# A diagonal mask moved from a matmul to VectorE, and one more job ahead of the emptying of a queue

## The chip, the cores and the metric

The kernel runs on one core of a Trainium2 chip. The metric is the time of one execution in device microseconds (us). Engines are named PE (TensorE's matmuls; PEld its weight loads), DVE (VectorE), ACT (ScalarE), POOL (GpSimd) and SP (SyncE, which issues the DMAs).

## The reference

One decoder layer for 2048 tokens of width 1024, behind 16 learned meta tokens. One input projection gives q, k, v, forget logits and a gate for 16 attention heads of width 64, and the input and gate of a pooling branch. The attention's logits are causal and carry a decay:

```
h = layer_norm(concat([meta, x]))
q, k, v, f_logit, g_att, u, g_pool = split(h @ w_in)
c = cumsum(log_sigmoid(f_logit + b_forget))
s = q_t . k_s / 8 + c_t - c_s            # where key s <= query t, else -inf
a = (softmax(s) @ v) * silu(g_att)
p = multiscale_pool(u) * silu(g_pool)
out = layer_norm(2 ** 0.25 * h + concat([a, p]) @ w_out)[16:]
```

Everything is float32. The kernel keeps that precision with three matmuls of split operands (high x high, high x low, low x high) where one would do.

## The kernel before, in words

Only SP's queue is ordered by the framework's scheduler. On PE, DVE, ACT and POOL the instructions run in the order in which the code issues them (`Ordered`, lines 78 to 95). All helpers issue through line 86, so the profile shows L86 for every engine, and instructions are told apart by the names of their tiles.

The first stage normalises the tokens, turns them, and projects v. The second stage (about 333 to 1358 us) is a list of 40 jobs: two of the pooling branch, then the 16 `qk_job`s (one per head) with gate and pooling jobs between them, and three gate jobs (`ga_job`) behind the last head. Each job runs chunks through `proj` (line 490): 8 steps of three matmuls into a tile named `d`, which has two buffers. A `qk_job` has five chunks of 416 or 412 columns, a `ga_job` four of 512. ACT and DVE empty `d`; a `ga_job`'s result goes through one tile `gst` to DRAM (`gd`).

While the jobs run, a second kind of work is strewn between the steps. For every head and every block of 128 queries the kernel needs the row maximum of q.k, which the attention later subtracts. `max_piece` (line 502) makes it: one or two matmuls (`mx<-ka,qa`) put up to 1024 columns of logits into an accumulator tile `mx`, of which there are two buffers; on the block's diagonal, 128 columns, a mask must be added; then DVE reduces the columns to one maximum (`mxs<-mx`). A head has 26 such pieces, 16 of them with a diagonal, and `max_end` (line 525) adds five entries: two maxima on DVE, a transposition on PE (`tr`), the split of the result (`mh`, `ml`) and its store. The entries wait in a queue `pend`. After every step `tick` (line 478) adds to a credit and issues an entry for each whole credit: at least 0.3 a step, and, while `sched["tail"]` is set, the entries left divided by the steps left, so that the queue is empty by then.

`run_jobs` (line 682) runs jobs from n0 to n1. It is called up to the first job behind the last head; then the rest of `later` (products of the pooling branch, put off by one chunk) and of `pend` is issued at once, the pools of the second stage are closed, and the attention's first tiles are set up: memsets of `ka`, `vt`, `vc`, `zo`, `qa`, and loads of keys, values and queries (`load_kv`, `load_q`). Then `run_jobs` runs the other two gate jobs, and the third stage, the attention with the output projection strewn in, begins with `emit_s` (`s<-qa,ka`). The fourth stage is the rest of the output projection and the last normalisation.

In the job list `last_qk` is 36 of 0 to 39, so three gate jobs, 37 to 39, follow the last head.

Of the kernel before, what the change touches and what calls it, by code (L numbers as in the profile page):

```python
# [9 lines left out]
F32 = mybir.dt.float32  # L10
F32R = mybir.dt.float32r
BF16 = mybir.dt.bfloat16
AF = mybir.ActivationFunctionType
ALU = mybir.AluOpType
AX = mybir.AxisListType

P = 128
# [4 lines left out]
KT = D // P  # L22
# [18 lines left out]
def kernel(  # L41
# [20 lines left out]
    nc = tc.nc  # L62
# [35 lines left out]
    nc = NC()  # L98
    mm = nc.tensor.matmul
# [33 lines left out]
    def pool(stack, name, **k):  # L133
        if k.get("space") is not DRAM:
            k["reuse_waits"] = "tile"
        return stack.enter_context(tc.tile_pool(name=name, bufs=1, **k))

    cpool = pool(ctx, "cpool", side="right")
    ident = cpool.tile([P, P], F32, tag="ident", name="ident")
    make_identity(mk_ident, ident)  # L140
    identb = cpool.tile([P, P], BF16, tag="identb", name="identb")
    nc.vector.tensor_copy(identb, ident)
    mask_q = cpool.tile([P, P], BF16, tag="mask_q", name="mask_q")
    nc.gpsimd.memset(mask_q, 0.0)
    nc.gpsimd.affine_select(
        out=mask_q, in_=mask_q, compare_op=ALU.is_ge, fill=NEG, base=0,
# [5 lines left out]
        out=mask_k, in_=mask_k, compare_op=ALU.is_ge, fill=NEG, base=0,  # L152
# [16 lines left out]
    def dense():  # L169
        return psd.tile([P, 512], F32, tag="d", name="d", bufs=2)  # L170
# [13 lines left out]
    def w_split(st):  # L184
        wh, wl = w_slots()
        split(wh, wl, st, nc.gpsimd)
        return wh, wl

    with ExitStack() as vscope:
# [219 lines left out]
        out=tri, in_=tri, compare_op=ALU.is_ge, fill=0.0, base=-1,  # L409
# [3 lines left out]
        out=tri, in_=tri, compare_op=ALU.is_ge, fill=0.0, base=0,  # L413
# [4 lines left out]
    for c0, c1 in CHUNKS:  # L418
        n = c1 - c0
        ps = dense()  # L420
        for k in range(KT):
# [4 lines left out]
            out=zc[:, :n], in_=ps[32 : 32 + H, :n], func=AF.Identity, bias=bf_t  # L426
# [45 lines left out]
    ka = qp.tile([66, L], F32R, tag="ka", name="ka")  # L472
# [3 lines left out]
    sched = {"credit": 0.0, "steps": 0, "hook": None}  # L476
# [25 lines left out]
    def max_piece(mx, i, p):  # L502
        lo, hi = max(112, 1024 * p), min(1024 * (p + 1), P * i + 256)
        base = 1024 * p

        def go():
            ps = psm.tile([P, 1024], F32, tag="mx", name="mx", bufs=2)
            v = lo
            while v < hi:
                e = min(hi, 512 * (v // 512 + 1))  # L510
                diag = e == P * i + 256
                mm(
                    ps[:, v - base : e - base], qa[:, NM + P * i : NM + P * (i + 1)],
                    ka[:, v - 112 : e - 112], start=True, stop=not diag,
                )
                if diag:
                    mm(ps[:, e - P - base : e - base], identb, mask_q, start=False, stop=True)
                v = e
            nc.vector.tensor_reduce(
                out=mx[:, p, i : i + 1], in_=ps[:, lo - base : hi - base], axis=AX.X, op=ALU.max  # L520
            )

        return go
# [138 lines left out]
    jobs = [others.pop(0), others.pop(0)]  # L662
# [5 lines left out]
    last_qk = max(n for n, j in enumerate(jobs) if j[0] is qk_job)  # L668
    sched["tail"] = False

    def fetch(n):
        return w_load(jobs[n][2]) if n < len(jobs) else None
# [9 lines left out]
    def run_jobs(n0, n1):  # L682
        for n in range(n0, n1):
            fn, a, _ = jobs[n]

            def mid():
                if n + 1 < len(jobs):
                    state["w"] = w_split(state["st"])
                    state["st"] = fetch(n + 2)

            w = state.get("w") or cur
            if fn is not qk_job:
                m = n
                steps = 0
                while m < len(jobs) and jobs[m][0] is not qk_job:
                    steps += 40 if jobs[m][0] is u_job else 32
                    m += 1
                sched["steps"] = steps + KT
                sched["tail"] = True
            fn(a, w, mid)  # L700

    run_jobs(0, last_qk + 2)
    while later:
        later.popleft()()
    while pend:
# [85 lines left out]
    load_q(0)  # L791
    fetched[0] = 1
    kvq.popleft()
    run_jobs(last_qk + 2, len(jobs))
    phase_a.close()

    phase_w = ExitStack()
# [345 lines left out]
    for i, tt in enumerate(order):  # L1143
# [12 lines left out]
        for q in range(parts):  # L1156
            qs = slice(D // parts * q, D // parts * (q + 1))
            nc.vector.scalar_tensor_tensor(
                out=yt[:, qs], in0=yt[:, qs], scalar=mv[:, 0:1], in1=g_bc[:, qs],
# [3 lines left out]
                out=yt[:, qs], in0=yt[:, qs], scalar=rs, in1=b_bc[:, qs], op0=ALU.mult, op1=ALU.add  # L1163
# [63 lines left out]
```

## Time and profile before

| | |
|---|---|
| median of 3 runs | 2393.3 us (2392.06 to 2394.99) |
| the profiled execution | 2390.21 us, its span 2388.5 us |
| granted TensorE clock, mean | 0.993 |
| instructions | 32719 |
| PE busy | 2321.6 us, 97% |
| DVE busy | 1431.6 us, 60% |
| ACT, POOL busy | 959.7 us, 718.1 us |

How to read the rows. A timeline row gives start and duration in us, the engine, the operation, `out<-in` by the tiles' names, and the shape; in brackets the idle time of the engine before it and what ended it. `x2` merges two equal neighbours. A matmul's end is modelled and lies past the next one's start, so costs on PE are read from start to start. A tile's row gives the number of instructions and their shortest, middle and longest duration in ns, and the first and last start.

### The profile page before, as it was taken

What the parts mean: (1) busy time and instruction counts of PE and PEld (TensorE: products, weight loads), DVE (VectorE), ACT (ScalarE), POOL (GpSimd) and SP (SyncE); (2) the same over time, 40 slices, a digit from 0 to 9 for tenths busy, and PEclk for the clock granted to TensorE, in tenths of its full rate; (3) what the DMA queues carried; (4) which work ended last, traced back from release to release, by engine and by line L of the source; (5) the groups of instructions that cost most, each with busy time, mean ns of one, the idle gap of its engine ahead of it and who ended that gap; (6) DMA issues with size and microseconds to landing.
All of it is one profiled execution on the core that took longest, in us unless ns stands there. A gap on an engine that the chain in (4) does not pass through costs nothing. (4 is left out here: it accounts for less than half of the span.)

```text
span 2388.5 us, 32719 instructions
## 1 busy us (share of the span) xinstructions
PE 2321.6 (97%) x11706; PEld 1922.0 (80%) x11706; DVE 1431.6 (60%) x2116; ACT 959.7 (40%) x1813; POOL 718.1 (30%) x528
## 2 busy tenths in 40 slices
PE   6999999999999999999999999999999999999998
PEld 5778798898988989888887767777777777776787
DVE  6641145644655456545535188787888878778357
ACT  4431221222212212121111387777778777776000
POOL 4730021212313404050001135353453535444000
PEclk8999999999999999999999999999999999999999
DMA  7853231222222222222212576575666657555955
GB/s 255 263 164 97 59 96 61 89 63 82 90 61 90 77 66 85 68 75 86 77 67 79 159 205 190 159 222 164 195 187 198 199 164 227 175 176 152 310 185 167
DMA packets 317506, 333.59 MB, mean 140 GB/s; under 512 B 27744, under 2 KB 241072, under 8 KB 317312
## 3 DMA queue, kind: packets, MB, share of 16 engines
q1 hardware_dynamic: 317344, 331.51, 45.5%
q8 instruction: 92, 1.51, 0.3%
q14 instruction: 70, 0.57, 0.1%
HBM read 207.43 MB, written 124.00 MB: 139 GB/s over the span
## 5 line engine op out<-in xcount | busy, mean ns | idle before, releaser
L86 PE MATMUL d<-hh,wh 128*128 128x412 f32 (+2 forms) x1472 | 561.2, 381 | 0.0
L86 PE MATMUL d<-hl,wh 128*128 128x412 f32 (+2 forms) x1472 | 538.6, 366 | 0.0
L86 PE MATMUL d<-hh,wl 128*128 128x412 f32 (+2 forms) x1472 | 538.6, 366 | 0.0
L86 DVE TENSOR_REDUCE mxs<-mx 128x1 f32<-128x912 f32 (+14 forms) x416 | 358.1, 864 | 279.7 <-PE mx L86 275.2
L86 DVE TENSOR_TENSOR pl<-s,ph 128x512 fp32r<-128x512 f32 (+2 forms) x576 | 374.6, 663 | 166.6 <-ACT s L86 153.5
L86 ACT ACTIVATE ph<-s 128x512 fp32r<-128x512 f32 (+2 forms) x576 | 334.6, 581 | 170.1 <-PE s L86 159.2
L86 PE MATMUL d<-wh,xm 128*128 128x512 f32 x1024 | 352.3, 400 | 5.1 <-DMA xm<-xa 5.1
L86 ACT ACTIVATE s<-s 128x512 f32<-128x512 f32 (+2 forms) x576 | 332.7, 578 | 0.0
L86 PEld LDWEIGHTS d<-hl,wh 128*128 128x128 f32 x1472 | 278.4, 189 | 23.1
L86 PEld LDWEIGHTS d<-hh,wl 128*128 128x128 f32 x1472 | 276.9, 188 | 23.5
L86 PEld LDWEIGHTS d<-hh,wh 128*128 128x128 f32 x1472 | 280.6, 191 | 18.2
L86 PE MATMUL s<-qa,ka 68*128 68x512 f32 (+4 forms) x704 | 258.1, 367 | 18.4 <-DVE pl L86 18.3
L86 POOL TENSOR_TENSOR wl<-wst,wh 128x1024 fp32r<-128x1024 f32 x40 | 96.2, 2405 | 576.0 <-ACT wh L86 575.9
L86 PE MATMUL s<-qb,kb 128*128 128x512 f32 (+4 forms) x704 | 244.8, 351 | 0.0
L86 PE MATMUL xo<-ph,vt 128*128 128x512 f32 (+3 forms) x640 | 232.9, 368 | 0.0
L86 POOL TENSOR_TENSOR tu<-ph 128x512 f32<-128x512 f32 x144 | 191.3, 1330 | 134.6 <-ACT ph L86 116.1
L86 PEld LDWEIGHTS d<-wh,xm 128*128 128x128 f32 x1024 | 192.3, 189 | 42.8 <-issue 4.9
L86 PE MATMUL yo<-pl,vt 128*66 128x512 f32 (+3 forms) x640 | 223.0, 365 | 0.5 <-ACT c L86 0.5
L86 PE MATMUL mx<-ka,qa 66*128 66x512 f32 (+5 forms) x704 | 200.2, 351 | 6.5 <-ACT qa L86 3.9
L86 PE MATMUL d<-wl,xm 128*128 128x512 f32 x512 | 204.3, 399 | 0.0
L86 PEld LDWEIGHTS s<-qa,ka 68*128 68x128 f32 (+1 forms) x704 | 127.7, 181 | 73.3 <-DVE pl L86 31.3
L86 PEld LDWEIGHTS mx<-ka,qa 66*128 66x128 f32 x704 | 133.0, 190 | 23.5 <-ACT qa L86 5.2
(140 smaller groups left out, 3049.2 us busy)
## 6 DMA issues: line engine op xcount, KB each, us to landing
xm<-xp SPq DMA_DIRECT2D x32, 1024.0 KB
xm<-xa SPq DMA_DIRECT2D x20, 1024.0 KB
vd<-vs SPq DMA_DIRECT2D x32, 512.0 KB
vt<-vd SPq DMA_DIRECT2D x64, 256.0 KB
qb<-kqd SPq DMA_DIRECT2D x64, 256.0 KB
xa<-am SPq DMA_DIRECT2D x32, 512.0 KB
xp<-pm SPq DMA_DIRECT2D x32, 412.0 KB
kqd<-lo SPq DMA_DIRECT2D x64, 206.0 KB
```

Of the source, the lines that this page charges most:

```text
L86: return in_order(f(*a, **k))
```

## The change

The mask that is added to the diagonal's 128 columns was a bfloat16 tile, added by a matmul with the identity matrix (`identb`) into the accumulator. It becomes a float32 tile that DVE adds to the accumulator in place, between the block's last matmul and its reduction. And the first call of `run_jobs` goes on to the second job behind the last head, `drain` being `last_qk + 3`; the steps over which `tick` spreads the entries are counted up to `drain` where that comes before the next head. One job is left for the second call.

```diff
-    mask_q = cpool.tile([P, P], BF16, tag="mask_q", name="mask_q")
+    mask_q = cpool.tile([P, P], F32, tag="mask_q", name="mask_q")
...
-                    ka[:, v - 112 : e - 112], start=True, stop=not diag,
+                    ka[:, v - 112 : e - 112], start=True, stop=True,
                 )
                 if diag:
-                    mm(ps[:, e - P - base : e - base], identb, mask_q, start=False, stop=True)
+                    d = ps[:, e - P - base : e - base]
+                    nc.vector.tensor_tensor(out=d, in0=d, in1=mask_q, op=ALU.add)
...
-                while m < len(jobs) and jobs[m][0] is not qk_job:
+                while m < len(jobs) and jobs[m][0] is not qk_job and m != drain:
                     steps += 40 if jobs[m][0] is u_job else 32
                     m += 1
-                sched["steps"] = steps + KT
+                sched["steps"] = steps if m == drain else steps + KT
                 sched["tail"] = True
             fn(a, w, mid)
 
-    run_jobs(0, last_qk + 2)
+    drain = last_qk + 3
+    run_jobs(0, drain)
     while later:
         later.popleft()()
     while pend:
         pend.popleft()()
...
-    run_jobs(last_qk + 2, len(jobs))
+    run_jobs(drain, len(jobs))
```

## The prediction, made before any run of the change

> **What bounds the kernel now.** I read the busy shares of the page first, then the windows around the change, then the timeline of single matmuls.
>
> ```profile
> PE 2321.6 (97%) x11706; PEld 1922.0 (80%) x11706; DVE 1431.6 (60%) x2116; ACT 959.7 (40%) x1813; POOL 718.1 (30%) x528
> 333.00:1275.50 942.50, 938.64 (x4814) 838.89 (x4813) 491.99 (x671) 180.60 (x352) 210.51 (x165) 1.00 0.24 77
> 1275.50:1301.30 25.80, 25.80 (x117) 20.66 (x116) 9.20 (x11) 3.73 (x6) 2.40 (x1) 1.00 0.20 67
> 1301.30:1311.80 10.50, 6.52 (x20) 3.20 (x18) 9.09 (x12) 1.13 (x2) 2.51 (x2) 0.70 0.18 66
> 1311.80:1358.20 46.40, 46.39 (x194) 37.56 (x195) 1.82 (x6) 5.38 (x9) 5.13 (x6) 0.96 0.41 124
> ```
>
> The window lines give length, then busy PE, PEld, DVE, ACT, POOL, the granted clock, the DMA share, GB/s. From 333 to 1301 (projections, with the row maximum's pieces strewn between) PE has work all the time and DVE half of it: 491.99 of 942.50. So an instruction taken from PE there is worth its slot, and one given to DVE is free as long as DVE keeps up. The exception is 1301.30 to 1311.80: the pieces left over when the queue is emptied behind the first job after the last head. There DVE is full (9.09 of 10.50), PE waits, and its granted clock falls to 0.70.
>
> **The mask's matmul, removed.** There is one per head and block of 128 queries, 256 in all.
>
> ```profile
> L86 PE MATMUL mx<-mask_q,identb x256: 230/231/330, 333.1 to 1310.1; 128*128 128x128 bf16 x128
> 601.93 0.34 PE L86 MATMUL mx<-ka,qa 66*128 66x384 f32 x1
> 602.12 0.23 PE L86 MATMUL mx<-mask_q,identb 128*128 128x128 bf16 x1
> 602.16 0.43 PE L86 MATMUL d<-hh,wh 128*128 128x412 f32 x1
> 602.43 0.35 PE L86 MATMUL d<-hl,wh 128*128 128x412 f32 x1
> 602.62 0.35 PE L86 MATMUL d<-hh,wl 128*128 128x412 f32 x1
> ...
> 1272.08 0.58 PE L86 MATMUL mx<-ka,qa 66*128 66x400 f32 x2
> 1272.50 0.35 PE L86 MATMUL d<-hh,wh 128*128 128x412 f32 x1
> ...
> 1274.77 0.22 PE L86 MATMUL mx<-ka,qa 66*128 66x128 f32 x1
> 1274.83 0.23 PE L86 MATMUL mx<-mask_q,identb 128*128 128x128 bf16 x1
> 1274.87 0.43 PE L86 MATMUL d<-hh,wh 128*128 128x412 f32 x1
> 1275.14 0.35 PE L86 MATMUL d<-hl,wh 128*128 128x412 f32 x1
> ```
>
> A matmul's listed duration overlaps the next, so I go by starts. An undisturbed projection matmul of 412 columns takes 0.187 us (602.43 to 602.62; longer runs give the third digit), 0.454 ns a column. From 601.93 to 602.43 are 0.50 us; 384 columns are 0.174 and 412 are 0.187, so 0.139 is the mask's. Of this 0.04 is its own slot (602.12 to 602.16); the rest makes the next projection matmul late (0.27 instead of 0.187). At the narrowest piece, 1274.77 to 1275.14, 0.37 - 0.058 - 0.187 = 0.125. Done for the pieces whose rows stand alone, the same subtraction gives 0.131 as the middle value, whatever the width. A piece without a mask has no such loss: 1272.08 to 1272.50 is 0.42 for 912 columns, which at 0.454 ns are 0.414. So I take the whole 0.131: the 248 masks that start before 1275.5 give 248 x 0.131 = **32.5 us**. Ends: 248 x 0.04 = 9.9, if only the slot goes, and 248 x 0.14 = 34.7. I take the upper part because the piece without a mask is the case after the change.
>
> The Trainium skill ("TensorE: Matmul & The Clock Gate", the section "Wait — 56ns, not 53.3ns?") has a 128-column matmul cost 55.6 ns, start to start, on a warm array. By that alone the masks would give 248 x 0.056 = 13.9 us and the total below would shrink by 18.6; the rows show more than twice the page's price, so I go by the rows.
>
> **The add on VectorE, new.** 256 adds of 128 columns, in and out of the accumulator, with the mask from SBUF. No such row exists; the nearest are these:
>
> ```profile
> 1312.52 0.28 DVE L86 SCALAR_TENSOR_TENSOR ml<-tr,mh 16x128 fp32r<-16x128 f32 x1 [0.77 <-ACT mh L86]
> L86 DVE TENSOR_REDUCE mxs<-mx x416: 280/1028/1226, 333.3 to 1311.2; 128x1 f32<-128x912 f32 x54, 128x1 f32<-128x1024 f32 x11, 128x1 f32<-128x128 f32 x10, 128x1 f32<-128x144 f32 x6
> 1361.45 0.69 DVE L86 TENSOR_TENSOR pl<-s,ph 128x512 fp32r<-128x512 f32 x1 [46.94 <-ACT s L86]
> 1362.74 0.57 DVE L86 TENSOR_TENSOR pl<-s,ph 128x400 fp32r<-128x400 f32 x1 [0.60 <-ACT s L86]
> ```
>
> Two inputs, one from the accumulator, 128 columns: 0.28. The same kind at 512 and 400 columns extrapolates to 0.69 - 384 x 0.00107 = 0.28. I take 0.29: 248 x 0.29 = 71.9 us, DVE goes from 52% to 60% of 942.5. Behind the add on DVE stand the piece's reduction and whatever comes next (the low halves of k and q, the pool branch's two products); who waits for them is PE, at the matmul that reuses the buffer, two pieces on. The tightest place of the undisturbed part:
>
> ```profile
> 409.67 1.44 DVE L86 TENSOR_REDUCE mxs<-mx 128x1 f32<-128x912 f32 x2
> 411.22 0.58 PE L86 MATMUL mx<-ka,qa 66*128 66x400 f32 x2
> ```
>
> The first of the two reductions ends 1.11 after 409.67, at 410.78; PE reuses its buffer at 411.22: 0.44 to spare. Of the other distances before the tail, worked out for all 416 reductions, eleven lie under 0.8 us. In a replay of all rows, pushed back by 0.29 an add, and with each masked piece 0.131 sooner, no PE start is reached; with 0.8 an add it costs 1.9 us. So the adds cost **0**; if the cover were gone, the excess over about 0.6 an add would go to PE. The float32 mask is built once, by two instructions of GpSimd at the very start, ahead of the first projection; I count 0.
>
> **Two jobs ahead of the emptying, pieces spread over both.**
>
> ```profile
> 1275.52 0.40 PE L86 MATMUL d<-hh,wh 128*128 128x512 f32 x1
> ...
> 1303.97 3.18 DVE L86 TENSOR_REDUCE mxs<-mx 128x1 f32<-128x912 f32 x3
> 1305.13 2.22 PE L86 MATMUL mx<-ka,qa 66*128 66x400 f32 x4 [1.45 <-DVE mxs L86]
> 1311.81 0.38 PE L86 MATMUL tr<-ident,mxs 128*16 128x128 f32 x1 [1.39 <-DVE mxs L86]
> 1312.84 0.63 PE L86 MATMUL d<-hh,wl 128*128 128x512 f32 x1
> 1313.27 0.63 PE L86 MATMUL d<-hh,wh 128*128 128x512 f32 x1
> ...
> 1336.18 0.60 ACT L86 ACTIVATE gst<-d 128x512 f32<-128x512 f32 x1 [4.96 <-PE d L86]
> 1341.74 0.60 ACT L86 ACTIVATE gst<-d 128x512 f32<-128x512 f32 x1 [4.96 <-PE d L86]
> 1358.18 0.39 PE L86 MATMUL s<-qa,ka 68*128 68x512 f32 x1
> ```
>
> After the last head 22 entries are queued: 17 pieces and five of the end. The old rule shares them over 104 steps but runs only 32 of them, at the floor of 0.3 a step, so 10 pieces go out and 7, with the end, are left for the burst. The new rule shares them over 64 steps, all of which run: 22/64 = 0.34 a step, nothing is left. A pair of pieces then comes every six steps, 4.2 us, for at most 1.11 + 1.22 + 0.29 = 2.6 us of DVE.
>
> From the first job's start at 1275.52 to the attention's first matmul at 1358.18 are 82.66 us. Needed at full rate: 3 jobs x 4 chunks x 5.56 (1336.18 to 1341.74) = 66.7; the 17 pieces, 12928 columns by the code (912 for each of blocks 8 to 14, their second parts 4480, block 15's 2064), x 0.454 ns = 5.9; the transpose 0.2. That leaves **9.9 us** of waiting, slow clock (0.43 between 1312.84 and 1313.27 instead of 0.23) and the last 8 masks. Ends: 0, if the burst only moves, and 9.9.
>
> What moves behind it: the memsets of the attention's tiles (1.81 us the longest, on GpSimd), the loads of its first keys, values and queries on SP's queue, and the pool branch's last product on DVE.
>
> ```profile
> 1310.35 1.81 POOL L86 MEMSET ka<- 2x2064 f32 x1 [4.59 <-PE mx L86]
> 1314.41 0.32 SPq L86 DMA_DIRECT2D ka<-kqd  x1
> 1317.13 0.59 SPq L86 DMA_DIRECT2D qb<-kqd  x1
> 1337.66 0.56 SPq L86 DMA_DIRECT2D vc<-vd  x1
> ```
>
> The first set is issued 2.6 to 5.9 us after the emptying ends, and one job is still 22.2 us of PE: 16 us for it to land. All loads ahead took until 1337.66, 26 us, between the stores of the gates that the queue waits for. Now the last of them (for later blocks) may come some us into the attention. I take 0. Lower bound of a loss 0; upper bound: the DMA share 0.41 over 46.4 us is 19 us of transfers, all uncovered.
>
> **Sum.** 32.5 + 9.9 = 42.4. Against the profiled execution, 2390.2 with a span of 2388.5, that makes 2347.8; the three runs' median, 2393.3, lies 3.1 above it, so **2351**.
>
> **Rivals.**
> A. Only the mask's own slot goes: the lateness of the next matmul stays with the change from a piece to the projection. 9.9 + 9.9 = 19.8, so 2373.5. For it: the lateness is seen on the projection matmul, not on the mask. Against: 1272.08 to 1272.50. 10%. By the 55.6 ns of the Trainium skill (the section named above) it would be 2369.5.
> B. Both gains, but the attention starts on late loads: some 5 us, 2356; at the bound of 19, 2370. For it: 22 us ahead instead of 46; against: the 16 us of the first set. 15%.
> C. The burst moves with the emptying (the last pieces meet the add on DVE, or a rest is left): 32.5 only, 2361. Against: the step count. 5%.
> D. Slower: the add is held up by GpSimd, as an operation with two SBUF inputs is:
>
> ```profile
> 1365.17 1.28 POOL L86 TENSOR_TENSOR acc<-ph 128x512 f32<-128x512 f32 x1 [6.25 <-ACT ph L86]
> 1365.61 0.69 DVE L86 TENSOR_TENSOR pl<-s,ph 128x512 fp32r<-128x512 f32 x1 [0.31 <-ACT s L86]
> 1373.54 1.29 POOL L86 TENSOR_TENSOR acc<-ph 128x512 f32<-128x512 f32 x1 [5.08 <-ACT ph L86]
> 1373.65 1.72 DVE L86 TENSOR_TENSOR wl<-wst,wh 128x512 fp32r<-128x512 f32 x1
> ```
>
> At 1.72 an add, the replay makes PE wait about 109 us: 2393.3 + 109 - 42 = 2460. It turns into a loss above some 1.4 us an add. Against: the operation beside GpSimd with one input in the accumulator took its plain 0.69, and GpSimd is busy in only 210.51 of 942.50 us. 4%.
>
> **How the numbers follow.** The forecast has 66%, A 10, B 15, C 5, D 4. Alone its range is 2346 to 2355 (0.12 to 0.14 a mask, the runs' spread of 3 us). A to C reach to 2374; the low end is 2345. Only D is no gain, and B, A and C all lie over 0.2% (4.8 us, about what can be told from no change) below 2393: faster 0.94, same 0.02, slower 0.04.
>
> **What would show it.** The profile after should have no bf16 mask matmul on mx and 256 DVE adds of near 0.29 us; the attention's first matmul near 1316 instead of 1358; a granted clock of 1.00 all the way there; no PE wait for mxs; a projection matmul behind every piece at 0.187. It is wrong if an add takes over 0.8 us, if projection matmuls behind masked pieces still take 0.27, or if PE's first waits in the attention name a load.

## The result, and the profile after

The changed kernel takes 2355.4 us (median of 4 runs, 2353.42 to 2356.81) against 2394.0 before (median of 4, 2392.06 to 2394.99): a ratio of 0.9843, 95% interval 0.9831 to 0.9855. The forecast was 2351, its range 2345 to 2374. The profiled execution has a span of 2351.7 us, 36.8 less than before.

The page of the changed kernel, then its windows: the projections up to the first gate job behind the last head, the two gate jobs with the strewn entries, and the last gate job (columns as in the prediction's windows).

```profile
PE 2289.3 (97%) x11450; PEld 1924.1 (82%) x11450; DVE 1501.9 (64%) x2372; ACT 959.9 (41%) x1813; POOL 716.8 (30%) x528
333.00:1256.00 923.00, 919.63 (x4604) 848.77 (x4604) 568.69 (x926) 182.65 (x355) 210.85 (x165) 1.00 0.25 80
1256.00:1281.00 25.00, 25.00 (x111) 20.50 (x110) 11.97 (x17) 3.12 (x5) 2.38 (x1) 1.00 0.16 58
1281.00:1297.00 16.00, 16.00 (x71) 12.93 (x71) 3.60 (x7) 2.35 (x5) 2.40 (x1) 1.00 0.14 51
1297.00:1320.40 23.40, 23.40 (x102) 18.96 (x101) 3.00 (x8) 3.08 (x6) 5.29 (x6) 1.00 0.67 174
```

256 matmuls have gone from PE and 256 instructions have come to DVE. The window with full DVE, idle PE and a clock of 0.70 is gone: PE is busy at 1.00 up to the attention. The rows of the mask's tile, of GpSimd and DVE side by side, and the starts that bound the last stages:

```profile
L86 DVE TENSOR_TENSOR mx<-mx,mask_q x256: 289/300/300, 333.1 to 1287.1; 128x128 f32<-128x128 f32 x128
...
602.17 2.41 POOL L86 TENSOR_TENSOR wl<-wst,wh 128x1024 fp32r<-128x1024 f32 x1
603.54 0.30 DVE L86 TENSOR_TENSOR mx<-mx,mask_q 128x128 f32<-128x128 f32 x1 [0.37 <-PE mx L86]
603.87 0.96 DVE L86 TENSOR_REDUCE mxs<-mx 128x1 f32<-128x768 f32 x1
...
1247.41 0.40 PE L86 MATMUL d<-hh,wh 128*128 128x512 f32 x1
1296.69 0.27 PE L86 MATMUL tr<-ident,mxs 128*16 128x128 f32 x1
1320.45 0.39 PE L86 MATMUL s<-qa,ka 68*128 68x512 f32 x1
```

An add takes 0.30 us, also in the middle of a GpSimd operation. The Trainium skill ("SBUF — State Buffer", "Who interferes with whom") has a VectorE instruction with at most one SBUF input not contend with GpSimd; the row at 603.54 agrees.

Where the 36.8 us went, from the first starts of `mx`, of the first gate job behind the last head, of `s`, and the last start of `yo` (us, one profiled execution each):

| stage | before | after | change |
|---|---|---|---|
| up to the first piece | 333.0 | 332.8 | -0.2 |
| projections, first piece to first gate job | 942.5 | 914.6 | -28.0 |
| three gate jobs and the rest of the pieces | 82.7 | 73.0 | -9.6 |
| attention | 847.1 | 848.6 | +1.5 |
| end | 183.2 | 182.6 | -0.6 |

### The profile page after: what moved, and what is told of

Its sections match the earlier page's. It is cut to its first block, busy times and chain, and to the rows that moved or that the text cites. A ratio compares the mean times of both kernels' runs of the same rounds, so it can differ in the third digit from the quotient of the medians.

```text
span 2351.7 us, 32595 instructions
## 1 busy us (share of the span) xinstructions
PE 2289.3 (97%) x11450; PEld 1924.1 (82%) x11450; DVE 1501.9 (64%) x2372; ACT 959.9 (41%) x1813; POOL 716.8 (30%) x528
## 4 chain that ended last, share of the span: by engine, by line
PE 89%; DVE 3%; DMA 3%; ACT 2%; issue 2%; POOL 1%; SPq 0%; DVEq 0%; ACTq 0%; POOLq 0%
PE d L86 61%; PE s L86 11%; PE yo L86 7%; PE mx L86 6%; PE xo L86 5%; POOL tu L86 1%; DVE pl L86 1%; PE tr L86 1%; ACT ph L86 1%; POOL araw L86 1%; DMA wst<-in_wout_dram 0%; ACT s L86 0%; DMA wu<-in_wut_dram 0%; DMA g_bc<-in_ln_in_g_dram 0%; DVE acc L86 0%
## 5 line engine op out<-in xcount | busy, mean ns | idle before, releaser
L86 PE MATMUL d<-hh,wh 128*128 128x412 f32 (+2 forms) x1472 | 543.8, 369 | 0.0
L86 DVE TENSOR_TENSOR mx<-mx,mask_q 128x128 f32<-128x128 f32 x256 | 76.6, 299 | 117.4 <-PE mx L86 115.0
```

The source lines that it names most:

```text
L86: return in_order(f(*a, **k))
```

## The experiments

Two theories, made after the result was known. **W**: the mask's matmul cost some 0.13 us of PE, but behind a last chunk of 128 or 144 columns some 0.06 stays, as so short a matmul doesn't cover the load of the next weights; the burst's 9.6 us are a gain of their own. **R**: the masks gave 0.131 each as forecast, and 4 to 5 us were lost by the second part or later. What suggested W are these rows of the changed kernel, the narrowest piece at its end:

```profile
587.47 0.22 PE L86 MATMUL mx<-ka,qa 66*128 66x128 f32 x1
587.53 0.40 PE L86 MATMUL d<-hh,wh 128*128 128x412 f32 x1
587.77 0.35 PE L86 MATMUL d<-hl,wh 128*128 128x412 f32 x1
587.95 0.34 PE L86 MATMUL d<-hh,wl 128*128 128x412 f32 x1
```

From 587.53 to 587.77 are 0.24, not 0.187. Taken over all pieces and grouped by their widths, the middle time beyond the columns (at 0.454 ns each) is 0.052 to 0.066 us where the last chunk has 128 columns, 0.053 where it has 144, and 0.001 to 0.011 where it has 256 or more.

The runs of each comparison had the kernel before beside them: 2391.9 in the first (experiments 1 to 4), 2391.4 in the second (5 to 8), 2392.1 in the third (9). The whole times expected in experiments 1 and 2 were reckoned from some 2394, so there the differences are what to compare.

**1. The mask alone.** The add on VectorE; the queue as before.

```diff
-    drain = last_qk + 3
+    drain = last_qk + 2
...
-                while m < len(jobs) and jobs[m][0] is not qk_job and m != drain:
+                while m < len(jobs) and jobs[m][0] is not qk_job:
-                sched["steps"] = steps if m == drain else steps + KT
+                sched["steps"] = steps + KT
```

> The mask goes to VectorE, the queue is emptied behind the first gate job as before. Theory W (the mask's matmul cost 0.13 us, but behind a last chunk of 128 or 144 columns some 0.06 stays because the next weights do not load in so short a time): up to the first gate job 28 us less, the burst about 1 us longer by its 4 adds and half a us shorter by its 4 masks, so about 28 us less than before, 2366. Rival R (the masks gave the full 0.131 each, 32.5, and the missing 4 to 5 us were lost elsewhere, by the second part or in the attention): about 32 less, 2362.

Measured 2364.2 us, ratio 0.9884 (0.9870 to 0.9897), 27.7 less. The projections took 914.6 us, the gate jobs 83.4, as against 942.5 and 82.7 before. So the masks' part is 28, and the burst, with its adds, is slightly longer. That is W's figure; the 32 of R are not reached.

**2. The queue alone.** The matmul stays. Seen against the changed kernel:

```diff
...
-                    d = ps[:, e - P - base : e - base]
-                    nc.vector.tensor_tensor(out=d, in0=d, in1=mask_q, op=ALU.add)
+                    mm(ps[:, e - P - base : e - base], identb, mask_q, start=False, stop=True)
```

> The mask stays a matmul, the queue is emptied behind the second gate job with its entries spread over both. Theory W: the tail gains 9.6 us as in the changed kernel, less the 8 masks that stay in it (about 1.0), and the attention loses at most 1.5: 7 to 9 us less than before, 2385 to 2387. Rival R (the second part is what gave less): 4 to 5 us less, 2389 to 2390.

Measured 2386.1 us, ratio 0.9973 (0.9962 to 0.9983): 5.9 less, between the two theories' figures. The stages decide: the projections are unchanged (942.5), the gate jobs take 74.0 instead of 82.7, which is 8.7 less and the 9.6 without its 8 masks; the attention takes 851.5 instead of 847.1 and returns half of it. The second part gave what was forecast; the attention's length is told of below.

**3. Even chunks.** The same columns, chunks and pieces, but each block's columns cut evenly; a piece is laid into its accumulator so that a cut falls on column 512.

```diff
+    def max_cuts(i):
+        n = P * i + 144
+        count = -(-n // 512)
+        step = -(-n // (16 * count)) * 16
+        at = [112 + min(n, step * c) for c in range(count + 1)]
+        pieces = (P * i + 255) // 1024 + 1
...
-        lo, hi = max(112, 1024 * p), min(1024 * (p + 1), P * i + 256)
-        base = 1024 * p
+        cuts = max_cuts(i)[p]
+        lo, hi, mid_ = cuts[0][0], cuts[-1][1], cuts[0][1]
+        base = mid_ - 512
```

> The changed kernel with the columns of each block cut evenly, so that no chunk but block 0's has fewer than 256 columns (as many chunks and pieces as before, the same columns). Theory W: the projection matmul behind the 64 chunks of 128 columns is no longer late by 0.057, 3.6 us less than the changed kernel, about 2351.5. Rival R2 (the lateness belongs to every last chunk of a masked piece, or to the add on VectorE): no change, 2355.

Measured 2353.9 us (ratio to before 0.9838, 0.9825 to 0.9852), against 2356.1 in experiment 4. The projections take 912.2 us instead of 914.6. The last matmul of the last block, 400 columns instead of 128, in the timeline of this kernel:

```profile
1284.54 0.35 PE L86 MATMUL mx<-ka,qa 66*128 66x400 f32 x1
1284.73 0.40 PE L86 MATMUL d<-hh,wh 128*128 128x512 f32 x1
1284.96 0.39 PE L86 MATMUL d<-hl,wh 128*128 128x512 f32 x1
```

The projection matmul takes its plain 0.23. In the stage 2.4 of the 3.6 us that W expected are there. Summed over the stage from start to start, the lateness of the projection matmuls falls by 2.9 us (7.2 to 4.3) and not by 3.6, as some of the new last chunks leave up to 0.015 each; and 0.5 us is lost again ahead of the pieces' first matmuls. The two whole times lie only 2.2 us apart and their intervals overlap, so the stage is the evidence, not the total.

**4. The changed kernel again**, on the same chip.

> The changed kernel once more, for comparison on the same chip: 2353 to 2357 by every theory.

Measured 2356.1 us (0.9849, 0.9836 to 0.9863); projections 914.6, gate jobs 73.0, attention 848.7: the stages return to 0.1 us.

**5 and 6. More adds.** Three and five adds of the mask for one.

```diff
-                    nc.vector.tensor_tensor(out=d, in0=d, in1=mask_q, op=ALU.add)
+                    for _ in range(3):
+                        nc.vector.tensor_tensor(out=d, in0=d, in1=mask_q, op=ALU.add)
```

> The changed kernel with the mask added three times over (the masked logits become three times as negative, the maximum is the same): 0.9 us of VectorE a masked piece instead of 0.3. Theory W with the prediction's replay (VectorE's queue has room, about 0.6 us at the tightest places): PE loses 2.5 us, so 2357 to 2360. Rival D (the adds already stand in PE's way, or each one more delays the release of its buffer): 512 x 0.3 = 154 us at the worst, anything above 2370 speaks for it.

> The same with five adds, 1.5 us a masked piece. By the prediction's replay VectorE now sets the pace where block follows block: PE loses 60 us, about 2415, a little above the kernel before; the waits of PE name mxs. Rival (the replay is too strict, VectorE's idle half absorbs it): 2360 to 2375.

Three adds: 2359.8 us, ratio 0.9867 (0.9852 to 0.9881), some 4 more than the changed kernel; the projections take 918.6, 4.0 more, for 512 x 0.30 = 154 us of DVE. Five: 2441.4 us, ratio 1.0208 (1.0193 to 1.0224); the projections take 997.7, 83.1 more, where the replay had 60. That is 2441 in all where 2415 was expected. PE's waits in the kernels with three and with five adds (us in total, times, longest), and the window of the projections with five:

```profile
PE mx L86 <- DVE mxs L86: 2.3, 4, 0.6
...
PE mx L86 <- DVE mxs L86: 39.9, 82, 1.5
...
333.00:1300.00 967.00, 915.54 (x4413) 800.26 (x4413) 808.61 (x1851) 174.56 (x341) 208.22 (x164) 1.00 0.23 73
```

With five adds DVE is busy 808.61 of 967 us and PE waits for the reductions. The listed waits are shorter than the loss, as a matmul's listed end lies past the next start. Taken from start to start, the time lost ahead of the pieces' first matmuls, where the buffer is reused, grows by 3.8 us with three adds and by 65 with five: nearly all of the 4.0, and most of the 83.1. So the single add is free because DVE's queue has room; at 0.9 us a piece it starts to cost, and between 0.9 and 1.5 the gain turns into a loss.

**7. All three gate jobs ahead of the emptying.**

```diff
-    drain = last_qk + 3
+    drain = last_qk + 4
```

> All three gate jobs run ahead of the emptying, so the attention's first loads have no job of PE's to land behind. Theory W (the 22 us of the third job cover them, in the changed kernel they cost nothing): PE now waits for the first set, 5 us of issue and some 3 of landing, and comes back at the lower clock: 8 to 14 us more than the changed kernel, 2364 to 2370. Rival B (the loads ahead of the attention matter little, as it is short of ACT and DVE there): no change, 2354 to 2358.

Measured 2368.9 us, ratio 0.9904 (0.9889 to 0.9919): 13.5 more than the changed kernel. The longest wait of PE, and the first attention matmul with what came before it:

```profile
PE s L86 <- DMA qa<-kqd: 12.4, 1, 12.4
...
1325.55 0.38 SPq L86 DMA_DIRECT2D ka<-kqd  x1
1327.42 0.89 SPq L86 DMA_DIRECT2D qa<-kqd  x2
1333.64 0.76 PE L86 MATMUL s<-qa,ka 68*128 68x512 f32 x1 [12.40 <-DMA qa<-kqd]
```

This is the price of the loads without cover: one wait of 12.4 us, and the first matmuls at the lower clock (0.76 instead of 0.39; the granted clock from 1333.6 to 1343 is 0.50). In the changed kernel no such wait is there.

**8. One job, all entries in it.**

```diff
-    drain = last_qk + 3
+    drain = last_qk + 2
```

> The queue is emptied behind the first gate job as before the change, but its 22 entries are spread over the 32 steps of that job. Theory W (the gain is that nothing is left for a burst, not the second job itself): a pair of pieces comes every 2.9 us and needs at most 2.6 us of VectorE, so nearly the whole gain stays: 2354 to 2358, and the attention's loads have two jobs ahead of them. Rival (the second job is needed: VectorE, with 0.3 us of add a piece, falls behind and PE waits): 3 to 6 us more, 2359 to 2362.

Measured 2355.4 us, ratio 0.9852 (0.9835 to 0.9868), the same as the changed kernel. The gate jobs take 73.5 us instead of 73.0. The first of them in this kernel:

```profile
1248.00:1272.00 24.00, 23.75 (x107) 19.30 (x106) 19.19 (x29) 3.70 (x6) 2.38 (x1) 1.00 0.19 62
```

DVE is busy 19.19 of 24 us and keeps up. What the burst cost comes back through the count of steps; the second job is one way to have enough of them, not the cause.

**9. A mask matmul twice as wide**, on the kernel of experiment 2. The mask's tile becomes 256 wide, its first half zeros.

```diff
...
-                    mm(ps[:, e - P - base : e - base], identb, mask_q, start=False, stop=True)
+                    mw = 2 * P if e - v >= 2 * P else P
+                    mm(ps[:, e - mw - base : e - base], identb, mask_q[:, 2 * P - mw :], start=False, stop=True)
```

> The kernel of the second experiment (mask by matmul, queue spread over two jobs) with the mask's matmul twice as wide where its chunk allows it: 256 columns, the first 128 of them zeros, in 11 of 16 blocks of each head. Theory W (of the 0.13 us of a mask only some 0.06 are its columns; the rest is the next projection's weight load, for which 128 columns are too short a cover): the wider matmul covers that load, its own slot grows by 0.058 and the lateness shrinks by as much; the same time as the second experiment within 2 us, 2384 to 2388, and the projection matmul behind it no longer takes 0.27. Rival R3 (a fixed cost of the change between bfloat16 and float32 operands, whatever the width): the lateness of 0.085 stays and 176 x 0.058 = 10 us are added, 2396.

Measured 2386.7 us, ratio 0.9977 (0.9968 to 0.9987): the time of experiment 2. Its timeline:

```profile
600.35 0.28 PE L86 MATMUL mx<-ka,qa 66*128 66x256 f32 x1
600.48 0.29 PE L86 MATMUL mx<-mask_q,identb 128*128 128x256 bf16 x1
600.52 0.44 PE L86 MATMUL d<-hh,wh 128*128 128x416 f32 x1
600.79 0.35 PE L86 MATMUL d<-hl,wh 128*128 128x416 f32 x1
```

600.35 to 600.79 are 0.44; 256 and 416 columns at 0.454 ns are 0.305, so the mask's is 0.135, what it was with half the columns. The projections stay at 942.9. A fixed cost on top of the columns would have added 10 us; that is excluded, as W has it. One part of W's expectation failed: the projection matmul behind still reads 0.27, and starts 0.04 behind the mask. The price 0.135 holds for the sum; where the rows divide it isn't where the work divides.

The rows of the weight loads (PEld) show the division better. First the narrow piece of the changed kernel, then the mask of 128 columns in the kernel before, then the one of 256:

```profile
587.47 0.19 PEld L86 LDWEIGHTS d<-hh,wh 128*128 128x128 f32 x1
587.58 0.19 PEld L86 LDWEIGHTS d<-hl,wh 128*128 128x128 f32 x1
587.77 0.19 PEld L86 LDWEIGHTS d<-hh,wl 128*128 128x128 f32 x1
...
602.12 0.20 PEld L86 LDWEIGHTS d<-hh,wh 128*128 128x128 f32 x1
602.24 0.19 PEld L86 LDWEIGHTS d<-hl,wh 128*128 128x128 f32 x1
...
600.48 0.20 PEld L86 LDWEIGHTS d<-hh,wh 128*128 128x128 f32 x1
600.60 0.19 PEld L86 LDWEIGHTS d<-hl,wh 128*128 128x128 f32 x1
```

Where nothing disturbs, a load starts together with the matmul ahead of it: the third load of the narrow piece at 587.77, as the matmul `d<-hl,wh` in the rows shown with theory W. The second load of each place starts later than the listed start of the matmul ahead: 587.58 against 587.53, 602.24 against 602.16, 600.60 against 600.52. The second projection matmul then follows 0.19 after that load. So the first projection matmul gets going, by this reading, only when the second load starts: 0.11 us after its own weights began to load behind the narrow chunk, and 0.12 behind the mask, whether that had 128 columns or 256. The middle values over all such pieces are 0.108 to 0.110 and 0.121 to 0.124. The wait goes with the load, not with the columns, as W has it.

## Why the prediction was right, and where it was off

The prediction held in its range and in its mechanism: two gains, no price for the adds, no wait for the loads. But 2355.4 lies at the upper edge of the 2346 to 2355 that it gave for the forecast alone, as one term of its sum was off.

The masks were the term that was mis-sized: 32.5 forecast, **28.0** measured. The step that failed is to take the whole 0.131 for every piece as what goes. At the narrowest piece, 0.37 - 0.058 - 0.187 = 0.125 is a right reading of the rows before, but it gave the chunk of 128 columns its 0.058 as if nothing but its columns counted once the mask was gone. Without the mask the chunk has to cover the load of the projection's weights itself: 587.47 to 587.77 is 0.30, of which 0.187 is the projection's, so the chunk holds PE for 0.113. The case chosen as the one "after the change" (1272.08 to 1272.50) ended on 512 columns and couldn't show it. There are 64 chunks of 128 columns and 16 of 144; some 0.057 each makes 4.6, the size of the 4.5 that are missing. A sign that the prediction named, a projection matmul at 0.187 behind every piece, therefore failed at these 80 of the 256 masked pieces. Summed from start to start, the columns of the stage are 901.6 us in both kernels; all other time, the masks' included, was 41.0 and is 13.0, which gives the 28.0 again. Rival A was the wrong reading of the same rows: behind wide chunks some 0.01 us or less stays.

By the 55.6 ns that the Trainium skill ("TensorE: Matmul & The Clock Gate", "Wait — 56ns, not 53.3ns?") gives for a matmul of 128 columns, an estimate of the gain would have been 13.9 us. The masks gave twice that. Experiment 9 says why: 128 columns more were free, so the price was not that of its columns.

The adds: 0.29 forecast, 0.30 measured; no PE wait for mxs in the changed kernel, as forecast. The replay had the order of the limits right but was lenient: 2.5 against 4.0 us at three adds, 60 against 83 at five. Rival D (adds held up by GpSimd) didn't happen.

The tail: 9.9 forecast, 9.6 measured; PE's granted clock is 1.00 and nothing is left at the emptying. Rival C is out. The loads: counted at 0, and PE waits for none at the attention's start. The cover was ample: uncovered, the first set costs a wait of 12.4 us (experiment 7), and one job is 22. Rival B's price (5 us, at its bound 19) was of the right size for the case that did not come.

Not in the sum: the attention's +1.5. The loads are not shown to be its cause: with the loads as early as before (experiment 1) it took 848.8, with two jobs ahead of them (experiment 8) 848.3, in the changed kernel 848.6. It took 851.5 and 851.2 in experiments 2 and 9, which keep the matmul and move the emptying, but also 851.6 with five adds and 850.9 in experiment 7, so it doesn't take the matmul. What goes with it is the granted clock. The trace shows it at half for 7 to 14 us of the attention in the seven executions of 847.1 to 849.4, and for 17 to 24 us in the four of 850.9 to 851.6. Whether that is the cause, and what sets it, stays open; each is one execution.

The forecast of 2351 also carried the 3.1 us by which the profiled execution before lay under its median; after, the profiled execution lies 2.0 under.

The best version here is that of experiment 3, by 2.4 us of its stage; its whole time is 2.2 us lower, with overlapping intervals.

## What to carry to other kernels

Price a matmul to be removed from the starts around it, not from its columns, and ask of its neighbours what the removed one had covered for them: a narrow matmul ahead of a weight load can hold its engine for longer than its columns say. Work moved to a half-idle engine is free only up to the slack of its tightest release, and that limit is quick to find by repeating the work. A burst that empties a queue is a question of the steps over which it was spread; spread it over the steps that really run, and look for what stands behind the emptying before moving it.

## What the runs showed of the hardware

Unexpected: a matmul of the identity with 256 bfloat16 columns between float32 ones cost PE 0.135 us, as with 128; and a float32 chunk of 128 columns, 0.058 us long by its columns, held PE for about 0.115 when a load of 128 x 128 weights followed. From 256 columns on (0.116 us) all but some 0.01 us was covered. That it is the weight load rests on the rows of the loads, which lie 0.11 to 0.12 us apart at all these places; the runs vary the widths, not the load itself.
